# Query projection of the attention split by token half: the second half moved behind the first attention steps

## The chip, the cores and the metric

One core of a Trainium2 chip runs one launch of the kernel. The metric is the device time of that launch in microseconds (us), as the median of several runs. All tensors are float32 in HBM. The engines are called as the profile calls them: PE (TensorE matmul), PEld (its weight load), DVE (VectorE), ACT (ScalarE), POOL (GpSimd) and SP (SyncE, here only an issuer of DMAs). Each engine works through its own queue, and semaphores order the engines against each other.

## What is computed

One encoder block over 1024 tokens of width 1024. A normalised input goes through one projection whose columns feed two mixers: windowed attention (8 query heads, 2 key/value heads, head width 64) and a bidirectional gated DeltaNet (4 heads, width 128, chunks of 64). Both go through one output projection, then a squared-ReLU feed-forward layer follows. Cut to what matters here:

```python
xn = _rmsnorm(h, norm_mix_w)                       # 1024 x 1024
q_a, k_a, v_a, qkv_g, z_g, a_g, b_g = split(xn @ w_in)
attn = _windowed_gqa(q_a, k_a, v_a, bias, in_window, sink)    # each block of 128 queries sees 3 blocks of keys
gdn  = _gdn_mixer(qkv_g, z_g, a_g, b_g, ...)       # inverts 64x64 triangles, then a scan over chunks, both directions
h = h + concat([attn, gdn]) @ w_out
h = h + square(relu(_rmsnorm(h) @ w_ffn_in)) @ w_ffn_out
out = _rmsnorm(h, norm_final_w)
```

The change concerns only when `q_a` (8 heads x 64 = 512 columns, so four column blocks of 128) is computed.

## The kernel before

Float32 precision is had from three matmuls. Each operand is split into a high part that TensorE's float32r type holds exactly and a low remainder; `mm3` (L136 to L138) issues high x high, high x low and low x high into one PSUM bank. A *gemm* below is one column block of 128 by one half of 512 tokens: 8 steps of K by 3 matmuls of 128x512, so 24 matmuls, all into one bank of `psA`. `split` makes the two parts of a weight: ACT casts the high part (L123), POOL subtracts it (L124). `load_w` brings the raw float32 weights as two tiles of `wr`.

SBUF is cut into pools of equal pages: `pg` (24 pages of 4 KB a partition), `dbl` (2 of 8 KB), `sc` and `wr` (4 of 4 KB each), `wh` and `wl` (3 of 4 KB each) and `pt` (12 of 2 KB). PSUM has four banks `psA` and four `psB`. A page is given again to a later tile when its last reader is done, so a tile waits for the page as well as for its data. In the names that the order prints, the last number is the tile's own, the one before it that of the page request (`psA_380_2803`).

The work is written as Python generators, each yielding a rough cost; `weave` takes the next piece from the stream that has used the smallest share of its weight. A scheduler then sets the final order of each engine's queue with a model of its own. On the chip each engine keeps to that order.

Around the change stand these pieces:

- `proj_conv`, `proj_z`, `proj_attn` (first stream of the first weave): the projections. The last eight gemms of `proj_attn` are the queries. For each key/value head `kv`, `pair` gives column block `i` and token `half` in the order (0,0), (1,0), (0,1), (1,1). After each gemm DVE scales the bank into `q` (L509), ACT casts the high part (L510), POOL makes the low part (L511), and SP writes both to a DRAM array `qad` (L513, two writes of 256 KB).
- `query(n, kv)` (L609): SP reads the queries of one block of 128 tokens back from `qad` in the layout that the scores need, two reads of 128 KB.
- `invert` in steps 0 to 3 (the inversion of the triangles): for each step SP loads a `dbl` page from the array `atd` (L721); PE makes products of 32x32 blocks (L738), ACT moves them (L741), PE makes the next ones (L749, L753), DVE and ACT put together `t64` (L758, L763, L765), PE makes 64x64 products from it and the `dbl` page (L774), ACT moves them (L776), PE makes the last products (L782), DVE places them (L785). Copies of the diagonal (L731) go beside it. Steps 0 and 1 stand in the first weave, steps 2 and 3 at the head of the second.
- `bias_table` (L541): 16 DMAs issued from ACT's queue, into `pg` pages that the normalised input held before.
- `attention`: for each block `n` of queries and each `kv`, scores (L556, L557) into four banks of `psA`, DVE adds the bias and takes the maximum (L558), ACT the exponentials (L570), DVE the normalisation (L575); two steps later the transposes (L585), ACT's copies of them (L587) and the products with the values (L597, DVE's copy L600).
- `scan`: the DeltaNet's chunks. Its first products are L820, followed by DVE's L838 and L839. It is woven with the attention.

In `phases` the first weave runs at 145 to 100, and the second, attention and output against inversion and scan, at 100 to 95.

## Time and profile before

| | |
|---|---|
| median of 3 runs | 1226.01 us (1224.49 to 1228.44) |
| the profiled execution: its own time | 1226.09 us |
| its span | 1224.0 us |
| mean granted TensorE clock | 0.989 |
| busy share of the span | PE 96%, DVE 70%, ACT 50%, POOL 46% |
| HBM traffic | 122.39 MB read, 63.49 MB written |

The time is that of the whole launch; the span is from the first to the last event of the profile, 2.1 us less. In rows of the timeline the first number is the start in us from the span's start, the second the duration; `x24` means 24 instructions told in one row, and the bracket says how long the engine had been idle and what released it. The `us` of an issue on a DMA queue (ACTq, SPq) is the queue's time, not that of the transfer. In rows by window, each engine has its busy time and its count of instructions, then follow the granted TensorE clock, the DMA share and GB/s. A PE matmul's busy time is longer than the distance to the next one, as matmuls overlap in the array; distances are told by starts.

### The profile page before, as it was taken

The page shows a single profiled execution, that of the slowest core. Times are in us where ns is not written, and L with a number is a line of the kernel's source. Part 1 is how long each engine was busy: PE and PEld are TensorE (multiplying, and loading weights), DVE is VectorE, ACT ScalarE, POOL GpSimd, SP SyncE. Part 2 cuts the span into 40 slices and gives each one's busy share as a digit, 9 for nine tenths or more (in the row PEclk, how much of TensorE's full clock was granted, in tenths as well). Part 3 has the DMA queues.
Part 4 walks back from the last instruction along what each step waited for, and adds up shares of the span by engine and source line. Part 5 has one row for each costly group of instructions (what it writes and reads, how often), then busy time and mean ns, then how long its engine had stood idle before and what let it go on. Part 6 is the DMA issues. An engine that isn't in the chain of part 4 may idle for free. (4 is left out here: it accounts for less than half of the span.)

```text
span 1224.0 us, 18445 instructions
## 1 busy us (share of the span) xinstructions
PE 1173.7 (96%) x6482; PEld 961.9 (79%) x6482; DVE 855.7 (70%) x1482; ACT 610.4 (50%) x1331; POOL 560.2 (46%) x470
## 2 busy tenths in 40 slices
PE   6999999899889999998999999999999999999997
PEld 5788878687768878887788888888878888888885
DVE  4676667993489996675855454453698796987976
ACT  6455688425376662124755454554555444344443
POOL 5354312224321233232764453635456565565695
PEclk9999999899989999999999999999999999999999
DMA  6134344433645577222144444344789534343323
GB/s 244 52 103 145 92 170 152 162 123 113 207 146 182 157 249 269 76 95 100 56 154 157 146 154 164 130 155 146 240 275 317 200 103 163 131 159 116 103 86 138
DMA packets 121629, 187.62 MB, mean 153 GB/s; under 512 B 11043, under 2 KB 64416, under 8 KB 121537
## 3 DMA queue, kind: packets, MB, share of 16 engines
q1 hardware_dynamic: 103876, 155.20, 38.4%
q10 hardware_dynamic: 17661, 31.24, 6.8%
q8 instruction: 51, 0.84, 0.3%
q14 instruction: 41, 0.34, 0.1%
HBM read 122.39 MB, written 63.49 MB: 152 GB/s over the span
## 5 line engine op out<-in xcount | busy, mean ns | idle before, releaser
L136 PE MATMUL psA<-pg,wh 128*128 128x512 f32 x416 | 165.0, 397 | 2.1 <-ACT pt L473 2.1
L138 PE MATMUL psA<-pg,wl 128*128 128x512 f32 x416 | 164.5, 395 | 0.0
L137 PE MATMUL psA<-pg,wh 128*128 128x512 f32 x416 | 164.2, 395 | 0.0
L124 POOL TENSOR_TENSOR wl<-wr,wh 128x512 fp32r<-128x512 f32 x44 | 66.8, 1540 | 156.5 <-ACT wh L123 128.7
L1194 DVE TENSOR_TENSOR pg<-pg 128x512 fp32r<-128x512 f32 x112 | 124.3, 1145 | 12.9 <-ACT pg L1193 12.9
L124 POOL TENSOR_TENSOR wh<-wr,wh 128x512 fp32r<-128x512 f32 x32 | 47.0, 1487 | 138.2 <-ACT wh L123 138.2
L1111 ACT ACTIVATE pt<-pt 128x512 f32<-128x512 f32 x64 | 40.3, 632 | 122.6 <-DVE pt L1101 122.6
L136 PE MATMUL psA<-pg,pg 128*128 128x512 f32 x256 | 98.7, 391 | 0.9 <-DVE pg L1239 0.9
L137 PE MATMUL psA<-pg,pg 128*128 128x512 f32 x256 | 99.2, 391 | 0.1
L138 PE MATMUL psA<-pg,pg 128*128 128x512 f32 x256 | 99.2, 389 | 0.0
L136 PEld LDWEIGHTS psA<-pg,wh 128*128 128x128 f32 x416 | 78.8, 190 | 19.5 <-ACT pt L473 2.4
L137 PEld LDWEIGHTS psA<-pg,wh 128*128 128x128 f32 x416 | 78.7, 189 | 17.9 <-issue 0.9
L138 PEld LDWEIGHTS psA<-pg,wl 128*128 128x128 f32 x416 | 78.7, 189 | 16.7
L124 POOL TENSOR_TENSOR pg<-wr,pg 128x512 fp32r<-128x512 f32 x48 | 73.2, 1559 | 37.9 <-ACT pg L123 37.9
L1193 ACT CAST pg<-pg 128x512 fp32r<-128x512 f32 x112 | 66.7, 620 | 36.4 <-DMA pg<-sd 31.3
L137 PE MATMUL psB<-pg,pg 128*128 128x512 f32 x192 | 74.9, 390 | 0.8 <-POOL pg L124 0.7
L136 PE MATMUL psB<-pg,pg 128*128 128x512 f32 x192 | 74.7, 389 | 0.0
L138 PE MATMUL psB<-pg,pg 128*128 128x512 f32 x192 | 74.7, 389 | 0.0
L123 ACT CAST wh<-wr 128x512 fp32r<-128x512 f32 x76 | 43.6, 623 | 52.1 <-PE psA L137 31.9
L1101 DVE TENSOR_TENSOR pt<-psB,pt 128x512 f32<-128x512 f32 x39 | 26.9, 690 | 57.6 <-PE psB L138 40.7
L1101 DVE TENSOR_TENSOR pt<-psA,pt 128x512 f32<-128x512 f32 x39 | 26.7, 689 | 51.3 <-PE psA L138 34.1
L136 PEld LDWEIGHTS psA<-pg,pg 128*128 128x128 f32 x256 | 48.0, 188 | 12.1 <-DVE pg L1239 2.1
(395 smaller groups left out, 3234.8 us busy)
## 6 DMA issues: line engine op xcount, KB each, us to landing
sd<-pt ACTq DMA_DIRECT2D x112, 256.0 KB, 2.1
pg<-sd SPq DMA_DIRECT2D x112, 256.0 KB, 2.9
wr<-in_w_ffn_in SPq DMA_DIRECT2D x32, 512.0 KB, 3.6
wr<-in_w_in SPq DMA_DIRECT2D x22, 512.0 KB, 4.2
pg<-in_x SPq DMA_DIRECT2D x16, 512.0 KB, 5.0
wr<-in_w_ffn_out SPq DMA_DIRECT2D x16, 512.0 KB, 4.7
sc<-kvd SPq DMA_DIRECT2D x14, 512.0 KB, 3.7
kvd<-pt SPq DMA_DIRECT2D x16, 256.0 KB, 2.4
```

The lines of the kernel that those rows point to most:

```text
L123: a = nc.scalar.copy(out=h, in_=raw)
L124: b = (eng or nc.gpsimd).tensor_tensor(out=l, in0=raw, in1=h.bitcast(F32), op=ALU.subtract)
L136: nc.tensor.matmul(ps, wh, xh, start=first, stop=False, skip_group_check=onto)
L137: nc.tensor.matmul(ps, wh, xl, start=False, stop=False, skip_group_check=onto)
L138: return nc.tensor.matmul(ps, wl, xh, start=False, stop=last, skip_group_check=onto)
L1101: self.nc.vector.tensor_tensor(out=out, in0=in0, in1=in1, op=ALU.add)
L1111: self.nc.scalar.activation(out=c, in_=c, func=AF.Relu)
L1193: nc.scalar.copy(out=s[:, 0], in_=raw)
L1194: v.tensor_tensor(out=s[:, 1], in0=raw, in1=s[:, 0].bitcast(F32), op=ALU.subtract)
```

## The change

The queries leave `proj_attn` and become `proj_query(half)`. Half 0 (tokens 0 to 511, the four column blocks) stays at the end of the first weave's first stream. Half 1 gets a weave of its own after `bias_table`, at weights 20.8, 14.8 and 18.2, with the inversion steps 2 and 3 and the first 12 pieces of the attention. The inversion steps 2 and 3 leave the head of the scan's stream.

The split weights have to last until half 1 has used them. Block (0,0) is kept in one `dbl` page, high and low part together; block (1,1) has its high part in two `pt` tiles and its low part in `wl`; blocks (0,1) and (1,0) are in `wh` and `wl` as before. Half 1 goes through the blocks in the order (0,0), (1,1), (0,1), (1,0). The number of gemms, casts, subtractions and DMAs of the queries is the same as before. Lines of the kernel before from L541 on stand 23 lines further down in the changed one (L774 is L797, L556 is L579, L820 is L843); the query's own lines L509, L510, L511 and L513 are L532, L533, L534 and L536.

```diff
--- before.py
+++ after.py
@@ -502,18 +502,41 @@
                 pv = self.transposed(t, 0)
                 nc.vector.tensor_copy(out=self.va[:, 4 * half:4 * half + 4, :], in_=pv)
             yield 5.2
-        for kv in range(2):
-            raws = self.load_w(self.w_cols(w, C_AQ + 256 * kv, 256))
-            for i, half, ps in self.pair(raws):
-                q, qh = self.pt(), self.pt(dt=F32R)
-                nc.vector.tensor_scalar(out=q, in0=ps, scalar1=0.125, scalar2=None, op0=ALU.mult)
-                nc.scalar.copy(out=qh, in_=q)
-                nc.gpsimd.tensor_tensor(out=q, in0=q, in1=qh.bitcast(F32), op=ALU.subtract)
-                for part, t in enumerate((qh.bitcast(F32), q)):
-                    nc.sync.dma_start(out=self.qad[kv, part, i, :, half * HALF:(half + 1) * HALF], in_=t)
-                if i == 1 and half == 0:
-                    self.qs.append(self.query(0, kv))
-                yield 5.2
+
+    def proj_query(self, half):
+
+        nc = self.nc
+        if half == 0:
+            self.wq = {}
+        for kv, i in (((0, 0), (0, 1), (1, 0), (1, 1)), ((0, 0), (1, 1), (0, 1), (1, 0)))[half]:
+            if half == 0:
+                if i == 0:
+                    raws = self.load_w(self.w_cols(self.io["w_in"][0], C_AQ + 256 * kv, 256))
+                if (kv, i) == (0, 0):
+                    both = self.dbl((P, 2, NK, P), F32R)
+                    high, low = [both[:, 0, a:a + 4, :] for a in (0, 4)], both[:, 1]
+                elif (kv, i) == (1, 1):
+                    high, low = [self.pt((P, 4, P), F32R) for _ in range(2)], self.wl((P, NK, P))
+                else:
+                    h, low = self.wh((P, NK, P)), self.wl((P, NK, P))
+                    high = [h[:, a:a + 4, :] for a in (0, 4)]
+                for kh in range(2):
+                    self.split(raws[kh][:, :, i * P:(i + 1) * P], high[kh], low[:, 4 * kh:4 * kh + 4, :])
+                self.wq[kv, i] = high, low
+            high, low = self.wq[kv, i]
+            ps = self.ps("psA")
+            for k in range(NK):
+                x = self.xt[half][k]
+                self.mm3(ps, high[k // 4][:, k % 4, :], low[:, k, :], x[:, 0], x[:, 1], k == 0, k == NK - 1)
+            q, qh = self.pt(), self.pt(dt=F32R)
+            nc.vector.tensor_scalar(out=q, in0=ps, scalar1=0.125, scalar2=None, op0=ALU.mult)
+            nc.scalar.copy(out=qh, in_=q)
+            nc.gpsimd.tensor_tensor(out=q, in0=q, in1=qh.bitcast(F32), op=ALU.subtract)
+            for part, t in enumerate((qh.bitcast(F32), q)):
+                nc.sync.dma_start(out=self.qad[kv, part, i, :, half * HALF:(half + 1) * HALF], in_=t)
+            if i == 1 and half == 0:
+                self.qs.append(self.query(0, kv))
+            yield 5.2
 
 
     def bias_rows(self):
@@ -1327,7 +1350,7 @@
         self.kc, self.qc = [None] * 4, [None] * 4
         self.qs = []
         self.wo, self.hnt, self.scanned, self.summed, self.rows = [{}, {}], [None, None], set(), [], {}
-        run(weave((chain(self.proj_conv(C_GV, "v"), self.proj_z(), self.proj_attn()), 145.0),
+        run(weave((chain(self.proj_conv(C_GV, "v"), self.proj_z(), self.proj_attn(), self.proj_query(0)), 145.0),
                   (chain(self.prep(), self.eliminate(), self.diag_blocks(), self.invert(tt, (0, 1))), 100.0)))
         self.bias_table()
 
@@ -1345,9 +1368,10 @@
 
         w_attn = {3: self.load_wout(0, (0,)), 5: self.load_wout(0, (1,)), 7: self.load_wout(0, (3,))}
         w_gdn = {1: self.load_wout(1, (0,)), 2: self.load_wout(1, (1, 2)), 4: self.load_wout(1, (3,))}
-        run(weave((output(), 100.0),
-                  (chain(self.invert(tt, (2, 3)), self.scan(0, tt[0], w_attn), self.load_wout(0, (2,)),
-                         self.scan(1, tt[1], w_gdn)), 95.0)))
+        out = output()
+        run(weave((self.proj_query(1), 20.8), (self.invert(tt, (2, 3)), 14.8), (itertools.islice(out, 12), 18.2)))
+        run(weave((out, 100.0),
+                  (chain(self.scan(0, tt[0], w_attn), self.load_wout(0, (2,)), self.scan(1, tt[1], w_gdn)), 95.0)))
         ng = DFF // 256
         self.norm_half(0)
         cols[1], rest[1] = self.columns(self.load_w1(1), 2)
```

What the scheduler makes of it can be seen in the queues. First PE's queue at inversion step 0. Before:

```order
L753 MATMUL psB_337_2377<-pt_335_2370,sc_327_2298 32x32
L136 MATMUL psA_380_2803<-pg_34_224,wh_378_2797 128x512
...
L138 MATMUL psA_380_2803<-pg_41_245,wl_379_2798 128x512
L774 MATMUL psB_351_2496<-pt_338_2426,dbl_331_2330 64x64 x16
L782 MATMUL psB_353_2515<-pg_332_2332,pt_352_2513 64x64
...
L424 MATMUL psB_358_2567<-ident_84,pt_357_2565 128x128 x4
L738 MATMUL psB_362_2580<-sc_323_2266,dbl_359_2573 32x32
...
L136 MATMUL psA_385_2841<-pg_34_224,wh_383_2835 128x512
```

Now:

```order
L776 MATMUL psB_337_2377<-pt_335_2370,sc_327_2298 32x32
L797 MATMUL psB_351_2496<-pt_338_2426,dbl_331_2330 64x64 x16
L805 MATMUL psB_353_2515<-pg_332_2332,pt_352_2513 64x64
...
L424 MATMUL psB_358_2567<-ident_84,pt_357_2565 128x128 x4
L761 MATMUL psB_362_2580<-sc_323_2266,dbl_359_2573 32x32
...
L136 MATMUL psA_379_2802<-pg_34_224,dbl_378_2797 128x512
```

All 24 matmuls of the first query gemm (`psA_380`) stood between the 32x32 products and the 64x64 products of step 0; now no gemm stands between them, and the first query gemm (`psA_379`, reading its weights from the page `dbl_378`) comes behind the first products of step 1's inversion. The page `dbl_378` is the one that `dbl_331`, step 0's own input, held: its last reader is L797.

Second, SP's queue where the attention's first queries are written and read back; `pt_407` and `pt_401` are the queries of (n 0, kv 1), `pt_428` and `pt_424` those of (n 1, kv 0). Before, the end of the gemms:

```order
L513 DMA qad_78<-pt_406_3014 128x512
L513 DMA qad_78<-pt_405_3013 128x512
L609 DMA pt_407_3020<-qad_78 64x4x128 x2
L513 DMA qad_78<-pt_410_3049 128x512
L513 DMA qad_78<-pt_409_3048 128x512
L609 DMA pt_428_3142<-qad_78 64x4x128 x2
```

Now:

```order
L632 DMA pt_387_2872<-qad_78 64x4x128 x2
L536 DMA qad_78<-pt_394_2911 128x512
L536 DMA qad_78<-pt_393_2910 128x512
L744 DMA dbl_477_3382<-atd_83 128x2x512 x2
L536 DMA qad_78<-pt_400_2950 128x512
L536 DMA qad_78<-pt_399_2949 128x512
L632 DMA pt_401_2956<-qad_78 64x4x128
L632 DMA pt_424_3088<-qad_78 64x4x128
L632 DMA pt_401_2956<-qad_78 64x4x128
```

The writes of the last gemm of half 0 (`pt_400`, `pt_399`) now stand behind the load of `dbl_477`, the input of inversion step 3. Its page is the one that holds the weights of block (0,0), whose last reader is that block's gemm of half 1, the last gemm ahead of the attention. The reads of the queries (0,1) and (1,0) stand behind those writes. Before, two further gemms followed on PE after the writes that the read of (0,1) needs.

Third, PE's queue from the scores of (1,0), `pt_428` before and `pt_424` now, to those of (1,1). Before:

```order
L556 MATMUL psA_440_3202<-pg_342_2444,pt_407_3020 128x256
L557 MATMUL psA_440_3202<-pg_344_2446,pt_407_3020 128x256
...
L556 MATMUL psA_450_3294<-pg_341_2443,pt_428_3142 128x384
...
L557 MATMUL psA_454_3307<-pg_343_2445,pt_428_3142 128x384
L774 MATMUL psB_463_3348<-pt_447_3279,dbl_429_3145 64x64 x16
L585 MATMUL psA_459_3330<-ident_84,wr_419_3108 128x128
L585 MATMUL psA_461_3337<-ident_84,wr_419_3108 128x128
L556 MATMUL psA_467_3369<-pg_342_2444,pt_444_3222 128x384
```

Now:

```order
L579 MATMUL psA_441_3198<-pg_341_2443,pt_424_3088 128x384
...
L580 MATMUL psA_445_3211<-pg_343_2445,pt_424_3088 128x384
L797 MATMUL psB_457_3284<-pt_438_3183,dbl_409_3011 64x64 x10
L608 MATMUL psA_450_3234<-ident_84,wr_415_3054 128x128 x2
...
L608 MATMUL psA_452_3241<-ident_84,wr_415_3054 128x128 x2
...
L797 MATMUL psB_457_3284<-pt_438_3183,dbl_409_3011 64x64
L136 MATMUL psA_454_3248<-pg_63_342,pt_395_2917 128x512
...
L138 MATMUL psA_454_3248<-pg_81_433,wl_397_2919 128x512
L797 MATMUL psB_457_3284<-pt_438_3183,dbl_409_3011 64x64 x5
L579 MATMUL psA_461_3305<-pg_342_2444,pt_435_3126 128x384
```

The gemm of block (1,1), half 1 (`psA_454`, weights in `pt_395` and `wl_397`), stands behind the scores of (1,0) and the first transposes, and its bank is the one of the third of those four scores.

The two gemms left stand further on in the same way: that of block (0,1), 24 matmuls, between the first value product (L620, tiles of n 0) and the scores of (2,0); that of block (1,0) between the scores of (2,1) and the transposes of (1,1), ahead of the last products of inversion step 3 and of the scan's first products (L843).

## The prediction

> **What bounds the kernel now.** I read the page's busy shares first, then windows of the stretch that the change touches, then the engines' timelines there.
>
> ```profile
> span 1224.0 us, 18445 instructions
> PE 1173.7 (96%) x6482; PEld 961.9 (79%) x6482; DVE 855.7 (70%) x1482; ACT 610.4 (50%) x1331; POOL 560.2 (46%) x470
> ```
>
> PE is the bound of the whole, so I ask where PE loses time around the queries, and whether the moved gemms could stand in those holes. Rows by window (length, PE, PEld, DVE, ACT, POOL busy, granted clock, DMA share, GB/s):
>
> ```profile
> 271.60:325.24 53.64, 52.69 (x491) 42.97 (x489) 18.84 (x36) 21.78 (x36) 23.39 (x23) 1.00 0.50 159
> 325.24:361.10 35.86, 28.50 (x545) 23.37 (x543) 29.69 (x105) 30.57 (x77) 9.88 (x12) 0.86 0.39 118
> 330.00:340.00 10.00, 4.58 (x49) 3.91 (x44) 7.47 (x31) 9.90 (x29) 1.70 (x2) 0.68 0.28 75
> 340.00:350.00 10.00, 10.00 (x133) 7.81 (x132) 7.45 (x26) 7.69 (x24) 2.58 (x3) 0.81 0.11 29
> 350.00:360.00 10.00, 8.09 (x164) 6.48 (x162) 9.44 (x32) 9.15 (x21) 1.71 (x3) 1.00 0.59 174
> 370.00:400.00 30.00, 29.44 (x217) 24.99 (x216) 27.96 (x103) 19.97 (x59) 5.62 (x4) 1.00 0.61 192
> ```
>
> The first row runs from the first query gemm to the first scores: PE is idle for 0.95 us of 53.64. The second runs from the first scores to the scan's first product: PE is idle for 35.86 - 28.50 = 7.4 us, and at a mean clock of 0.86 it loses another 0.14 x 35.86 = 5.0 us of array time, 12.4 in all at most, some of it counted in both. So there are holes for about two gemms. But they have an owner: in 350 to 360 DVE is busy 9.44 of 10 and ACT 9.15, and to 400 DVE 27.96 of 30. Behind the first scores it is the softmax's engines that set the pace.
>
> **Prices of the moved work.** The release of the last gemms shows the period and the steps that follow each gemm:
>
> ```profile
> 315.57 0.62 ACT L510 CAST pt<-pt 128x512 fp32r<-128x512 f32 x1 [5.04 <-DMA pg<-biasd]
> 320.91 0.62 ACT L510 CAST pt<-pt 128x512 fp32r<-128x512 f32 x1 [4.72 <-DMA pg<-biasd]
> 325.24 0.28 PE L556 MATMUL psA<-pg,pt 128*128 128x256 f32 x1
> 325.50 0.69 DVE L509 TENSOR_SCALAR pt<-psA 128x512 f32<-128x512 f32 x1 [4.67 <-issue]
> 326.98 1.28 POOL L511 TENSOR_TENSOR pt<-pt,pt 128x512 f32<-128x512 f32 x1 [4.07 <-ACT pt L510]
> 319.55 3.60 SPq L609 DMA_DIRECT2D pt<-qad  x2
> qad<-pt SPq DMA_DIRECT2D x13, 256.0 KB, 2.9
> pt<-qad SPq DMA_DIRECT2D x14, 128.0 KB, 4.5
> DMA to landing us min/median/max: 2.4/4.1/7.6
> ```
>
> One gemm is 320.91 - 315.57 = 5.34, say 5.4 us of PE. It drags DVE 0.69, ACT 0.62, POOL 1.28 and two SP writes along; a write lands after 2.9 us and a read back after 4.5 (medians of 300 to 340 us, by the two rows of issues); the last row is for all transfers of `qad`, writes and reads together. The change keeps the count of all of these. The weights' casts and subtractions are as many as before and go beside gemms, on ACT and POOL that are busy 21.78 and 23.39 of 53.64 us: nothing, as long as gemms cover them.
>
> **First term: inversion step 0 loses its cover.** PE, then ACT, then DVE:
>
> ```profile
> 270.36 0.24 PE L749 MATMUL psB<-sc,pt 32*32 32x32 f32 x4 [0.49 <-ACT pt L741]
> 271.60 0.50 PE L136 MATMUL psA<-pg,wh 128*128 128x512 f32 x1
> 277.27 1.15 PE L774 MATMUL psB<-pt,dbl 64*64 64x64 f32 x32
> 279.11 1.15 PE L782 MATMUL psB<-pg,pt 64*64 64x64 f32 x32 [0.69 <-ACT pt L776]
> 280.77 1.09 PE L738 MATMUL psB<-sc,dbl 32*32 32x32 f32 x64
> 281.79 0.50 PE L136 MATMUL psA<-pg,wh 128*128 128x512 f32 x1
> ...
> 270.20 2.68 ACT L763 COPY pt<-sc 32x256 f32<-32x256 f32 x4
> 272.90 2.69 ACT L731 COPY pg<-sc 32x256 f32<-32x256 f32 x4
> 275.62 1.27 ACT L497 CAST pg<-pt 64x512 fp32r<-64x512 f32 x2
> 276.79 1.25 ACT L498 CAST pg<-pt 64x512 fp32r<-64x512 f32 x2
> 278.47 0.59 ACT L776 COPY pt<-psB 128x512 f32<-128x512 f32 x1 [0.43 <-PE psB L774]
> ...
> 273.73 0.42 DVE L765 TENSOR_SCALAR pt<-psB 32x256 f32<-32x256 f32 x1
> ```
>
> From 271.60 to 277.27 PE now does the first query gemm, and under it ACT and DVE make the operand of L774. The changed order has no gemm there: the first one must wait for its weights' page, which L774's successor (L797) frees. So L797 starts at about 273 and can't end before DVE's last part at 274.15, some 275.3; ACT's copy behind it still stands behind the four casts, which end at 278.04, so the products behind it start at about 278.7. That is 1.4 + 3.4 us of idle PE, and the clock falls after that. The clock's price is seen elsewhere in this trace:
>
> ```profile
> 906.50 0.50 PE L136 MATMUL psB<-dbl,sc 128*128 128x512 f32 x1 [2.08 <-ACT pt L1106]
> 907.10:910.40 3.30, 3.30 (x9) 2.62 (x8) 2.57 (x5) 2.85 (x6) 1.28 (x1) 0.50 1.04 389
> ```
>
> An idle of 2.08 us was followed by a stretch of some 3.3 us at a granted clock of 0.50. I take 1.4 us for it here. Then L805, the transposes and L761 take from 278.7 to 281.6, with the clock to 283.0, where the first gemm starts. Before, the second began at 281.79. The deficit is 5.4 + 1.2 = 6.6 us. [...]
>
> Three gemms later PE meets a second new wait: the weights of block (1,1) are cast only behind the third gemm's own cast in ACT's queue. Gemm end, 0.69 + 0.62 + one cast of 0.62 make about 1.9 us. So five gemms end, and the first scores start, at 283.0 + 5 x 5.4 + 1.1 (inversion step 2's first products, done early) + 0.6 (a small rest of step 1) + 1.9 + small losses, which I put at 317.6: 7.6 us before the old 325.24, with three gemms, 16.2 us, still owed. If nothing of these were hidden, the kernel would be 16.2 - 7.6 - 1.1 = 7.5 us slower; if the whole 12.4 of the holes took them, 4.9 faster.
>
> **Second term: the attention's start.** The rows that set it before:
>
> ```profile
> 335.62 0.45 PE L774 MATMUL psB<-pt,dbl 64*64 64x64 f32 x2 [3.93 <-ACT pt L763]
> 339.84 0.67 PE L556 MATMUL psA<-pg,pt 128*128 128x384 f32 x1
> 348.88 0.44 PE L556 MATMUL psA<-pg,pt 128*128 128x384 f32 x1
> 349.52 2.00 DVE L575 TENSOR_SCALAR wr<-wr,nm 128x384 f32<-128x384 f32 x3
> 359.96 1.75 DVE L575 TENSOR_SCALAR wr<-wr,nm 128x384 f32<-128x384 f32 x3
> 361.11 1.16 PE L820 MATMUL psB<-sc,pg 128*128 128x128 f32 x8
> ```
>
> The hole that a gemm could fill is the 3.93 us ahead of L774. In the new order it opens sooner and a gemm doesn't fill it. The reads of query (0,1) were issued at 319.55, under two further gemms that covered write, landing, read and landing. Now the last gemm of half 0 ends just ahead of the first scores; from 317 on DVE 0.69, ACT 0.62 and POOL 1.28 make its parts, the write lands 2.9 later, the read 4.5 after that: 317 + 0.7 + 0.6 + 1.3 + 2.9 + 4.5 = 327.0, and SP has the load for step 3 ahead of them. The scores of (0,1) then start at 327.4, those of (1,0) at about 330.5 and the gemm behind them at 334, since its bank is freed by DVE's pass over the third of those scores. So PE stands nearly idle from about 319 to 327, more than in the hole it had. That gemm ends at 334 + 5.4 = 339.5, and the scores of (1,1) follow, which stood at 339.84 before. Everything gained by starting 7.6 us early is used up: -0.3 us, with one gemm done and two owed. From both sides: with landings between the shortest, 2.4 us, and the medians that I used, and some delay of DVE, the gemm starts between 331.5 and 335, so -2.8 to +0.7.
>
> **Third term: the two gemms left, 10.8 us.** One stands ahead of the scores (2,0), which began at 348.88, the other ahead of the transposes before the scan. DVE is the engine to be fed there, at 9.44 of 10. While PE does a gemm, DVE can only live on what it already has. At 348.88 that was about L575's 2.00 and the 0.69 of a value copy; of 5.4 + 0.7 us until the new scores DVE then starves some 3.4. At the second it has more, an L575 of 1.75 and the bias pass of the last scores, and starves some 2. The three gemms' own evictions add 3 x 0.69 = 2.1 to DVE. Sum +7.5; ends +2.1 (no starving) and +10.8 (no cover). I take 7.5 since DVE had at most 0.6 us of slack per 10 there.
>
> **Fourth term: the clock behind the hole.** The 330 to 350 rows with 0.68 and 0.81 say that about 3.2 + 1.9 = 5.1 us of array time went at half rate. Of it some 2 us fell behind 339.84. The new hole comes earlier; the clock is back for the scores (1,1), but the gemm at 334 may run part of its time at half rate. I take -2.0 + 1.3 = -0.7, with -2 and +0.7 as ends.
>
> **The sum.** -0.3 + 7.5 - 0.7 = +6.5 us at the scan's start, which is 6.5 against the 7.5 of nothing hidden. From there to 400 DVE has 2 us of slack in 30, so little is won back, and the queues behind are those of before. On the profiled execution's own 1226.09 us that is 1232.6; the median of the runs, 1226.01, is 0.08 away, so no correction: 1232.5.
>
> **Rivals.**
>
> *Holes filled (faster).* The mechanism is the gemms taking the place of waiting in the attention's first steps. It decides at the third term: if DVE's backlog covers both gemms (third term +2.1), the gemm of (1,1) starts at 331.5 (-2.8) and the half clock goes (-2.0), the sum is -2.7; and if PE's 12.4 us can all be taken, -4.9: about 1222. For it speaks the 7.4 us of idle PE. Against it: PE's order is fixed, and each gemm stands ahead of scores that DVE waits for, not beside them. The point is 7.5 us hidden of the 16.2.
>
> *Little difference.* The third term at about half, +4, with -2.8 from quick landings: +1 us or so, 1227. For it speaks that DVE's queue holds work of three attention steps at once; against it the 0.69 us evictions, which are sure.
>
> *Wait for the queries worse than priced (slower still).* SP's step 3 load, ACT's bias DMAs and the writes share the queues' order. If the reads land at 7.6 us, the longest of this trace, 3 us more are lost ahead of the gemm: 1235.5, and up to 1239 with both gemms bare.
>
> *The change doesn't move anything* is excluded: the queues show the moved gemms.
>
> **How the numbers follow.** A median of three runs that spread over 1224.49 to 1228.44 can't tell less than about 0.3%, 3.7 us, from no change. My forecast with its sizes, and the worse wait, are slower by more than that: 0.44 and 0.12. The cases between -3.7 and +3.7 get 0.25, the filled holes 0.19. So faster 0.19, same 0.25, slower 0.56. The range reaches down to 1219, below the filled holes' 1222 by the size of one landing, and up to 1239; the likeliest case alone would be 1229 to 1237.
>
> **What would show it.** First: no gemm at 271.6, two idles and a granted clock of 0.50 near 276 to 283, the first gemm at about 283. Second: first scores at 316 to 319, then idle PE until the scores of (0,1) at 326 to 328, released by the read from `qad`; the gemm of (1,1) at 332 to 335. Third: DVE idle ahead of the bias passes of (2,0), and the scan's first product at 366 to 371 in place of 361.11. I am wrong if that product comes before 363, if the DVE doesn't starve beside the two late gemms, or if the time is lost or won behind 400.

## Result, and the profile after

| kernel | median us | runs | ratio to before, 95% interval |
|---|---|---|---|
| before | 1227.22 | 4 | |
| changed | 1248.12 (1247.09 to 1251.05) | 4 | 1.0172 (1.0156 to 1.0188) |

The change costs about 21 us. The forecast was 1232.5 us with a range to 1239: the direction was right, the size a third. The profiled execution of the changed kernel took 1251.05 us, 3 us above the median; its trace is 25 us longer than that of before, and that is the difference accounted for below. So some 4 us of it belong to that execution rather than to the change.

The page's busy shares of the changed kernel, same columns as before:

```profile
span 1249.0 us, 18445 instructions
PE 1185.5 (95%) x6482; PEld 967.6 (77%) x6482; DVE 858.9 (69%) x1482; ACT 610.0 (49%) x1331; POOL 559.1 (45%) x470
```

As many instructions as before on every engine, and DVE, ACT and POOL are within 3.2 us of their old busy times. PE alone is busy 11.8 us longer with the same 6482 matmuls. Now both traces cut at the same events: inversion step 0, the first scores, the scores of (1,1), the scan's first product, a cut in the feed-forward part, and the end. Rows by window (length, PE, PEld, DVE, ACT, POOL busy, granted clock, DMA share, GB/s), before:

```profile
268.80:325.24 56.44, 55.00 (x649) 45.07 (x649) 20.39 (x40) 24.46 (x41) 25.58 (x24) 1.00 0.51 165
325.24:339.84 14.60, 9.18 (x220) 7.91 (x218) 11.54 (x46) 12.46 (x32) 4.61 (x6) 0.79 0.41 125
339.84:361.11 21.27, 19.33 (x328) 15.46 (x326) 18.16 (x60) 18.11 (x46) 5.28 (x6) 0.91 0.38 113
361.11:640.00 278.89, 265.50 (x1572) 221.76 (x1569) 212.22 (x547) 132.88 (x341) 108.25 (x95) 0.99 0.46 152
640.00:1215.90 575.90, 571.82 (x2490) 466.49 (x2488) 394.77 (x471) 268.91 (x476) 321.48 (x228) 1.00 0.48 162
```

And changed:

```profile
268.50:318.92 50.42, 43.89 (x641) 35.73 (x641) 16.39 (x33) 21.66 (x37) 18.64 (x18) 0.86 0.35 107
318.92:345.29 26.37, 15.82 (x186) 13.06 (x184) 15.17 (x54) 13.00 (x37) 8.69 (x10) 0.74 0.50 152
345.29:379.80 34.51, 30.92 (x370) 23.12 (x368) 22.81 (x65) 21.89 (x53) 10.37 (x10) 0.90 0.34 112
379.80:664.90 285.10, 270.77 (x1570) 225.00 (x1567) 211.37 (x542) 130.50 (x332) 105.80 (x93) 0.98 0.46 150
664.90:1240.80 575.90, 571.14 (x2491) 465.38 (x2489) 394.60 (x471) 269.62 (x476) 320.73 (x228) 1.00 0.48 162
```

The last row is the same in both, 575.90 us. In the four rows ahead of it the length grows from 371.2 to 396.4, by 25.2 us. PE's idle time (length less busy) grows from 22.2 to 35.0, by 12.8; PE's busy time grows from 349.0 to 361.4, by 12.4, for the same work. By this account the loss is half waiting, half the same matmuls at a lower granted clock, and it lies in all four stretches. The account says where PE's time went; it doesn't say what the time would be at full clock, since a PE that does its matmuls faster may only wait longer.

The hole behind the first scores, on PE, ACT and SP of the changed kernel:

```profile
329.19 0.28 PE L772 MATMUL psB<-sc,pt 32*32 32x32 f32 x4 [8.84 <-ACT pt L764]
331.96 0.55 PE L579 MATMUL psA<-pg,pt 128*128 128x256 f32 x1 [1.71 <-DMA pt<-qad]
...
319.42 5.45 ACTq L564 DMA_DIRECT2D pg<-biasd  x5
324.90 1.28 ACT L590 ACT_TABLE_LOAD   x1 [4.89 <-DMA dbl<-atd]
328.77 0.36 ACT L764 COPY pt<-psB 128x256 f32<-128x256 f32 x1
...
320.09 1.62 SPq L536 DMA_DIRECT2D qad<-pt  x2
327.69 1.91 SPq L632 DMA_DIRECT2D pt<-qad  x3
```

Two waits end within 3 us of each other. ACT's five bias issues take 5.45 us, and the last of them goes out at 324.6, right behind the landing of step 3's input. That load was issued at 319.12, behind the last reader of the page with block (0,0)'s weights. The exponentials and the copy for step 2 stand behind ACT's issues. And the queries (0,1) are written at 320 to 321.7, read from 327.7 and landed at 331.9.

In the changed kernel's trace the granted clock stood at 0.50 for 10.24 us from 272.03, 3.41 from 306.16, 13.65 from 323.23 and 6.83 from 350.53. Rows of three pairs of neighbouring stretches of that trace:

```profile
347.12:350.53 3.41, 1.49 (x31) 1.21 (x30) 2.85 (x11) 3.17 (x6) 0.55 (x1) 1.00 0.58 192
350.53:353.95 3.42, 3.09 (x76) 1.99 (x76) 2.02 (x5) 3.41 (x13) 0.17 (x1) 0.50 0.02 5
...
538.27:541.68 3.41, 1.49 (x8) 1.11 (x8) 3.41 (x8) 1.24 (x2) 1.85 (x2) 1.00 0.40 131
541.68:545.09 3.41, 3.14 (x10) 2.66 (x11) 2.92 (x7) 0.62 (x1) 1.80 (x2) 0.50 0.27 104
...
272.03:275.45 3.42, 1.84 (x28) 1.71 (x30) 2.51 (x6) 3.34 (x6) 0.31 (x1) 0.50 0.29 80
275.45:278.86 3.41, 1.30 (x24) 1.12 (x22) 0.00 (x0) 3.36 (x7) 2.68 (x3) 0.50 0.00 0
```

Each of the two stretches in which PE was busy 1.49 us of 3.41 is followed by one at 0.50, and the one at 0.50 with 1.84 us busy by another at 0.50. No single idle in these stretches was longer than 2.10 us.

### The profile page after: what moved, and what is told of

The parts are those of the page before. It is cut to its first block, busy times and chain, and to the rows that moved or that the text cites. A ratio compares the mean times of both kernels' runs of the same rounds, so it can differ in the third digit from the quotient of the medians.

```text
span 1249.0 us, 18445 instructions
## 1 busy us (share of the span) xinstructions
PE 1185.5 (95%) x6482; PEld 967.6 (77%) x6482; DVE 858.9 (69%) x1482; ACT 610.0 (49%) x1331; POOL 559.1 (45%) x470
## 5 line engine op out<-in xcount | busy, mean ns | idle before, releaser
L138 PE MATMUL psA<-pg,wl 128*128 128x512 f32 x400 | 158.3, 396 | 0.0
L136 PE MATMUL psA<-pg,wh 128*128 128x512 f32 x384 | 152.8, 399 | 2.1 <-ACT pt L473 2.1
L137 PE MATMUL psA<-pg,wh 128*128 128x512 f32 x384 | 151.6, 395 | 0.0
L124 POOL TENSOR_TENSOR wl<-wr,wh 128x512 fp32r<-128x512 f32 x40 | 61.5, 1559 | 150.5 <-ACT wh L123 127.1
L138 PEld LDWEIGHTS psA<-pg,wl 128*128 128x128 f32 x400 | 75.7, 189 | 16.2
L136 PEld LDWEIGHTS psA<-pg,wh 128*128 128x128 f32 x384 | 72.9, 190 | 19.8 <-ACT pt L473 2.4
L137 PEld LDWEIGHTS psA<-pg,wh 128*128 128x128 f32 x384 | 72.9, 190 | 16.7 <-issue 0.9
```

The costliest lines, as they stand in the source:

```text
L124: b = (eng or nc.gpsimd).tensor_tensor(out=l, in0=raw, in1=h.bitcast(F32), op=ALU.subtract)
L136: nc.tensor.matmul(ps, wh, xh, start=first, stop=False, skip_group_check=onto)
L137: nc.tensor.matmul(ps, wh, xl, start=False, stop=False, skip_group_check=onto)
L138: return nc.tensor.matmul(ps, wl, xh, start=False, stop=last, skip_group_check=onto)
```

## Experiments

All ratios are to the kernel before on the same chip. The median beside each is that of its own runs.

**Order by halves alone, nothing late.**

```diff
- chain(..., self.proj_attn(), self.proj_query(0))          # first weave
+ chain(..., self.proj_attn(), self.proj_query(0), self.proj_query(1))
- run(weave((self.proj_query(1), 20.8), (self.invert(tt, (2, 3)), 14.8), (islice(out, 12), 18.2)))
- run(weave((out, 100.0), (chain(self.scan(...)...
+ run(weave((out, 100.0), (chain(self.invert(tt, (2, 3)), self.scan(...)...
```

> Only the order by halves and the new places of the weights are kept: all eight gemms stand ahead of the attention again, the inversion steps 2 and 3 at the head of the scan's stream. Theory A (three separate losses: about 8.6 us of PE until the first scores, of which 6.6 at inversion step 0; about 7.6 us in the hole behind the first scores; the rest behind it): only the first is left, 1233 us, with no gemm at step 0 and no wait above 5 us behind the first scores. Theory B (nearly all comes from the attention's start, the hole at step 0 is made up later): 1227 to 1229 us.

1235.84 us, ratio 1.0078 (1.0050 to 1.0106). The first scores start at 337.7 in place of 325.2; behind them the distance to the scan's first product is 35.0 us against 35.9. So the order by halves and the new places of the weights cost 9.5 us before a single gemm is late. That is theory A's side, with a first loss larger than its 6.6 and a time 3 us above its 1233.

**Step 0 covered again.** The double page goes to block (0,1); block (0,0) is in `wh` and `wl`.

```diff
- if (kv, i) == (0, 0):                      # takes the double page
+ if (kv, i) == (0, 1):
- ((0, 0), (1, 1), (0, 1), (1, 0)))[half]
+ ((0, 1), (1, 1), (0, 0), (1, 0)))[half]
```

> The changed kernel, but block (0,1) is kept in the double page and block (0,0) in wh and wl, so that the first query gemm has its weights without waiting for step 0's page. The queue of PE behind it is nearly that of the changed kernel. Theory A: the 24 matmuls stand at step 0 again, the idle and the half clock there go, 6 us less than the changed kernel, 1241 to 1242 us. Theory B: the first scores start 6 us sooner but the hole behind them grows by as much, 1247 us. A third way, that the page rather than the place matters: less than 3 us.

1246.71 us, ratio 1.0176 (1.0134 to 1.0217): no gain that could be told. The gemm is back at step 0, but the first scores start only 3.3 us earlier (315.6), and the hole behind them stands as it was (7.9 + 2.3 us). The time is that of the third way of its expectation, and of theory B too; the trace speaks for the third, since the hole didn't grow and PE waits 3.8 us for step 2's input ahead of the first scores.

**The same cover, with all gemms ahead**, tells what took its place.

> The order by halves with all eight gemms ahead of the attention, as in the first run, but block (0,1) in the double page and block (0,0) in wh and wl, so that the first gemm is at inversion step 0 again. If the 9.5 us of the first run are the bare step 0 with its idle and half clock, they go but for about 1.5 us of the new wait for the casts of block (1,1): 1226 to 1229 us. If they come from the places of the weights or from the queries' order otherwise: 1232 us or more.

1232.45 us, ratio 1.0036 (1.0017 to 1.0055): by the ratios 5 of the 9.5 us come back, 4.4 don't. The time is at the edge of the expectation's second case (1232 or more, by the places of the weights), though about half came back as the first case had it. PE's waits in this kernel between step 0 and the first scores (us in all, times, longest):

```profile
PE psB L761 <- DMA dbl<-atd: 4.8, 2, 2.8
PE psB L805 <- ACT pt L799: 1.0, 2, 0.7
```

PE waits 4.8 us for step 2's input from DRAM, a wait that the kernel before doesn't have. With one of the two `dbl` pages holding weights from step 0 until the first gemm of half 1, the inversion has one page left, and its next load starts only when the step before has read its own. So the double page costs the inversion its second buffer. In the changed kernel itself PE has no such wait ahead of the first scores (step 2's input is issued at 296.14 and first used at 303.66); there the page shows as step 0's lost cover and as the late load of step 3.

**One and two gemms late instead of three.** `late` is the generator of half 1, of which one or two pieces more are run ahead of the weave.

```diff
+ late = self.proj_query(1)
+ run(itertools.islice(late, 1))              # 2 in the second run
- run(weave((self.proj_query(1), 20.8), ...
+ run(weave((late, 20.8), ...
```

> The changed kernel, but the second gemm of half 1, block (0,0) being the first, is put ahead of the attention: its generator is run one piece ahead of the weave, which puts two of the four gemms of half 1 (blocks (0,0) and (1,1)) ahead of the first scores. Two gemms stay behind. Theory A (the hole behind the first scores is a wait for queries written, read back and for ACT, which a gemm in that place covers): 5 us less than the changed kernel, 1243 us. Theory C (what costs is each gemm that stands ahead of scores that DVE waits for, some 5 us for each): 1243 us too, but the hole stays and the late gemms get cheaper. The trace tells: the wait ahead of the scores of (0,1), 11.9 us in the changed kernel, is below 7 by A and above 10 by C.

> As the run with one piece ahead, with two pieces: three gemms of half 1 stand ahead of the first scores, only block (1,0) stays behind. Theory A: the hole behind the first scores falls to the old one, about 3.9 us, and what is left is step 0 and one late gemm: 1234 to 1236 us. Theory C: 1237 to 1239 us, about 5 us below the run with one piece ahead.

With two late gemms 1242.22 us (1.0127; 1.0098 to 1.0156), with one 1236.31 (1.0078; 1.0050 to 1.0105). In a row: none late 1235.8, one 1236.3, two 1242.2, three 1248.1. With two late the time fits theory A and theory C alike (1243); its trace fits A, since PE waits 4.0 us ahead of the scores of (0,1), not above 10. With one late it is between the two. The first scores start at 327.8, 324.3 and 318.9 with one, two and three late, but the scores of (1,0) at 334.7, 334.2 and 334.4: they are pinned. In all three PE waits there for queries from `qad`: 2.2 us ahead of (1,0) with one late, 4.0 and 1.7 us ahead of (0,1) with two and three. A gemm taken from ahead of the first scores makes those start earlier, not the next ones; so the first is free, and each further one costs 5.9 us, its own 5.4 and a little.

And one gemm late with step 0 covered:

> As the run before this one, but with the last gemm of half 1 left behind the first scores and the inversion steps 2 and 3 in the weave of the changed kernel. One gemm behind the scores was worth +0.5 us with the bare step 0, so 1227 to 1230 us; below 1224 only if a single late gemm fills the old hole of 3.9 us.

1233.82 us, ratio 1.0054 (1.0032 to 1.0077), no better than with none late and the same cover (1232.45), and above its expectation for the same reason, the wait for step 2's input (1.6 + 3.2 us in its trace).

**The late gemms cut to one step of K.**

```diff
+ nk = 1 if half == 1 and (kv, i) != (0, 0) else NK
- for k in range(NK):
+ for k in range(nk):
```

> The changed kernel, but the three gemms of half 1 that stand behind the first scores do one step of K only, 3 matmuls in place of 24, some 4.7 us of PE less each (part of the queries is left out); what follows each gemm is kept. If these gemms are bare where they now stand (theory C), 14 us less, 1234 us. If half of them is hidden in PE's holes, 7 us less, 1241 us. If the holes take them whole, 1246 to 1248 us. Theory A, by which the early start gains nothing, needs the first of these.

1235.74 us, ratio 1.0067 (1.0043 to 1.0091): 12.4 us less than the changed kernel for some 14 us of PE taken away. That is the first case of its expectation: the late gemms were nearly bare where they stood.

**The two waits of the hole.** Bias tables in 4 DMAs from an array of 128 stored rows a head:

```diff
- self.biasd = d("biasd", (8, 32, 512))
+ self.biasd = d("biasd", (8, P, 512))
- for m in range(4): ...  ap=[[511, 32], [32 * 512, 2], [1, 3 * P]]
+ ap=[[511, P], [P * 512, 2], [1, 3 * P]]
```

> The changed kernel, but the attention's bias tables come in 4 DMAs of ACT's queue rather than 16, from an array of bias rows that is stored four times as often; the result is the same. In the changed kernel the last of the 16 was issued only when the load of step 3's input had landed, at 324.9 us, and ACT's exponentials and the copy that step 2's products wait for stood behind it. Theory A1 (ACT held by these issues is the floor behind the first scores): step 2's products start at 323 to 325 us rather than 329.2 and the time falls by 4 to 5 us to 1243 to 1244. Theory A2 (the floor is the queries' way through DRAM): the products start sooner too, but the scores of (0,1) stay at 331 to 332 us and the time falls by less than 1.5 us.

1257.34 us, ratio 1.0250, slower. The larger array spoiled the test: PE lost 9.9 us in one wait that ended at 183.4 us. From PE's waits of that run (us in all, times, longest) and DVE's timeline:

```profile
PE psB L674 <- DVE pt L683: 9.9, 1, 9.9
...
182.26 1.12 DVE L683 SCALAR_TENSOR_TENSOR pt<-pt,cc,psB 128x128 f32<-128x128 f32 x4 [12.09 <-DMA biasd<-pt]
```

DVE's L683, for which PE waits, was itself released by the landing of that write, issued at 139.3. The write's source is a tile of `pt`, and L683 writes a tile of `pt`: so it most likely waited for the source's page. SP's other issues were slow in that stretch too (two loads of weights took 19.95 us of its queue, 5.56 in the changed kernel). The next run's expectation put the loss down to SP's queue, so there the write goes out from POOL's:

> The changed kernel with 4 bias DMAs of ACT's queue, as before, but the larger array of bias rows is written from POOL's queue: written from SP's it held SP's other transfers for some 10 us at 144 to 190, which hid what was asked. Theory A1 (ACT held by the issues): counted from the first scores to the end, 4 us less than the changed kernel, 1243 to 1245 us. Theory A2: less than 1.5 us. If the write still holds other transfers, the time is above 1250 us and only the stretch behind the first scores can be compared.

1258.64 us, ratio 1.0255, against 1257.34 and 1.0250 with the write on SP's queue: another queue didn't help. In both only the stretch behind can be compared: from the first scores to the scan's first product it is 58.5 us, against 60.9 in the changed kernel. By that ACT's hold is worth 2.5 us, which two spoiled runs suggest but don't show.

The queries of three steps from an array written long before (other values, same work):

```diff
+ arr = self.ktd[2 * kv:2 * kv + 2] if 0 < 2 * n + kv < 4 else self.qad[kv, part]
- src = self.qad[kv, part, :, :, n * P:(n + 1) * P]...
+ src = arr[:, :, n * P:(n + 1) * P]...
```

> The changed kernel, but the queries of (0,1), (1,0) and (1,1) are read from an array of equal shape that was written long before (the keys of the other mixer), so that these reads wait for no write; the values are others, the work is the same. Theory A1: the scores of (0,1) start right behind those of (0,0), but the exponentials and step 2's products stay at about 329 us, less than 2 us gained. Theory A2: 4 to 5 us gained, 1243 to 1244 us. If neither wait alone is the floor, both this run and the one with 4 bias DMAs gain little, and both together gain 6 us or more.

1239.95 us, ratio 1.0097 (1.0065 to 1.0129): 8.2 us less than the changed kernel, more than any theory gave. The scores of (0,1) start at 325.9 rather than 332.0. The stretch from the first scores to the scan is 55.4 us, 5.5 shorter. The clock goes with it: PE's rows are 14.40 busy of 24.10 us at 0.86 from the first scores to (1,1), and the next stretch to the scan runs wholly at 1.00. The first scores start 1.8 us earlier, which the edit doesn't touch; so the 8.2 is not all its own.

```profile
317.10:341.20 24.10, 14.40 (x185) 11.85 (x183) 14.82 (x54) 13.19 (x37) 8.73 (x10) 0.86 0.55 167
341.20:372.50 31.30, 28.55 (x373) 22.32 (x369) 22.65 (x65) 22.32 (x53) 10.40 (x10) 1.00 0.37 123
```

Both edits together:

> The changed kernel with both: 4 bias DMAs and the three early queries read from the array written long before. Theory A (the hole behind the first scores is made of these two waits, each hiding the other): the hole of 8.8 us goes to below 4, the gemm of block (1,1) starts at 330 to 333 us rather than 339.1, and the time is 1240 to 1242 us. Theory C (the hole only moves, since DVE and ACT need the time and each late gemm costs its 5 us wherever it stands): 1245 us or more.

1252.56 us, ratio 1.0204, with the same spoiled start; from the first scores to the scan 56.7 us, against 55.4 with the early queries alone. So the queries' way through DRAM was the main floor (A2).

**The clock alone.** 30 matmuls that no result uses, behind the bias passes of the first scores:

```diff
+ idle = self.ps("psB")
+ nc.tensor.matmul(idle[:, 0:4], self.ident, mx, start=True, stop=True)
+ for _ in range(30):
+     nc.tensor.matmul(idle, self.kh[0][:, 0:P], self.kh[0][:, 0:HALF], start=True, stop=True)
```

> The changed kernel with 30 matmuls of 128x512 added that no result uses, ordered behind the bias passes of the first scores, where PE is idle for 8.8 us. Theory D (half of the loss is the clock: between 268.5 and 664 us the changed kernel has 11.0 + 6.4 us of PE time lost at half rate against 3.3 + 1.5 before): the stretch at half rate from 323.2 to 336.9 goes, 3 us less, 1244 to 1246 us, though PE does 6.8 us more. Theory E (the clock costs nothing of its own, ACT and DVE pace these stretches): no less than 1247.5 us, and more if the added work delays the next products.

1245.00 us, ratio 1.0147 (1.0125 to 1.0169), 3.1 us less than the changed kernel though PE does 6.8 us more. The three stretches to the scan:

```profile
268.50:316.60 48.10, 40.88 (x593) 33.11 (x583) 16.93 (x32) 20.80 (x36) 18.73 (x18) 0.93 0.36 112
316.60:343.00 26.40, 23.05 (x218) 19.01 (x217) 15.17 (x53) 12.98 (x37) 8.35 (x9) 0.87 0.49 153
343.00:376.80 33.80, 30.13 (x370) 22.63 (x368) 22.85 (x65) 22.27 (x53) 10.63 (x10) 0.95 0.35 114
```

The clock there is 0.87 and 0.95 where it was 0.74 and 0.90, and the time is the one that theory D named. But the two rows that the added work touches are together only 0.7 us shorter than in the changed kernel (26.40 and 33.80 against 26.37 and 34.51), and the first row, which it doesn't touch, is 2.3 us shorter at a clock of 0.93 against 0.86. The intervals of the two ratios overlap as well. So it isn't shown that the half rate behind the first scores costs time of its own: the row in which the clock rose most, from 0.74 to 0.87, kept its length.

**Late gemms that take no page.** The kernel before, by columns, with its last gemms left out of the first weave; `wh` and `wl` hold their weights anyway.

```diff
+ attn = self.proj_attn()
- chain(..., self.proj_z(), self.proj_attn())
+ chain(..., self.proj_z(), itertools.islice(attn, 12 - late))         # late = 0, 1 or 2
- run(weave((output(), 100.0), (chain(self.invert(tt, (2, 3)), self.scan(...)...
+ out = output()
+ run(weave((islice(out, 3), 3.9), (self.invert(tt, (2,)), 7.4), (attn, 5.2)))  # 5, 6.5 and 10.4 with two
+ run(weave((out, 100.0), (chain(self.invert(tt, (3,)), self.scan(...)...
```

> The control for the two runs with late gemms: the same weave, the first three pieces of the attention with inversion step 2, then the rest, with no gemm moved. If the weave alone does nothing, 1226 to 1228 us; what the runs with one and two gemms give is to be read against this one.

> The kernel before, order by columns, weights in wh and wl as before; only the last query gemm is left out of the first weave and woven with the first three pieces of the attention and inversion step 2. It comes behind the scores of (0,0) and ahead of those of (0,1). No page is taken from the inversion. Theory F (the double page, not the moving, is what costs at the inversion; the hole behind the first scores is 3.9 us idle and about 3.4 us of half rate, and one gemm fills part of it): 1222 to 1226 us, no wait for the inversion's input from DRAM. Theory C (each gemm put behind the scores costs its 5 us): 1231 us.

> The same with the last two gemms, over five pieces of the attention; one comes behind the scores of (0,0), one behind step 2's 64x64 products, ahead of the first transposes. Theory F: within 3 us of the run with one gemm; theory C: 5 us above it, 1236 us. The first scores start 10.8 us earlier than in the kernel before where nothing else changes.

The weave alone: 1239.41 us (1.0089; 1.0064 to 1.0114), 11 us slower than before, a control that was not neutral (its PE waits 5.5 us ahead of step 2's last products). One gemm late: 1236.02 (1.0074; 1.0049 to 1.0098). Two: 1224.06 (0.9968; 0.9952 to 0.9984). Neither theory had that: F put two within 3 us of one, C 5 us above. The control differs from the run with two in its weave as well (three pieces of the attention against five), so the 15 us between them can't be put down to the gemms. Against the kernel before, two late gemms in this order cost nothing. Its rows to the scan:

```profile
268.50:311.60 43.10, 39.72 (x514) 32.14 (x515) 18.97 (x34) 21.40 (x36) 20.36 (x20) 0.96 0.41 134
311.60:340.10 28.50, 25.87 (x296) 21.52 (x294) 18.32 (x62) 15.39 (x40) 10.39 (x11) 0.94 0.54 164
340.10:359.60 19.50, 16.93 (x311) 13.06 (x309) 15.27 (x46) 15.80 (x37) 4.65 (x6) 0.91 0.46 149
```

The first scores start at 311.6, 13.6 us earlier than before, but the scores of (1,1) at 340.1 (339.8 before) and the scan at 359.6 (361.1): the gemms moved into idle time that the earlier start opened, and nothing behind came sooner. To see whether the small gain is real, and whether the place counts (the second run below is the same kernel with `(attn, 5.2)` in place of 10.4):

> The same kernel as the run with two late gemms, to narrow its interval. If the gain is real, the ratio to the kernel before stays at 0.995 to 0.999; if it was the draw of the runs, 0.999 to 1.002.

> Two late gemms as before, but the second one further back: behind the scores of (2,0) rather than ahead of the first transposes. Theory C (a gemm ahead of scores and transposes that wait costs its time): 2 to 5 us slower than the other place, 1226 to 1229 us. If DVE's backlog covers it there, the same time.

Again 1225.36 us, ratio 0.9988 (0.9976 to 1.0001); further back 1227.24, 0.9996 (0.9981 to 1.0012). Two gemms late are free there. The two runs of the one kernel, 22 executions, both lie below 1, by 0.3% and 0.1%, and the second is in the band that its expectation gave to a real gain; one of the two intervals reaches 1, so a gain of some 2 us is likely, not shown. The place of the second gemm makes 1.9 us between the medians and 0.0008 between the ratios, whose intervals overlap: theory C's 2 to 5 us and no difference can't be told apart.

## Why the prediction was right and wrong

The sign and the route of the first three terms held; the sum was a third of the loss. What failed is the size of the second and third terms, the clock term, and the nothing that was set behind the scan's start.

*First term, inversion step 0.* Its times were right: the first gemm was forecast at 283.0 and starts at 282.09, the first scores at 317.6 and start at 318.92; the wait for block (1,1)'s cast, 1.9, is 1.73. PE's timeline of the changed kernel there:

```profile
272.84 0.44 PE L797 MATMUL psB<-pt,dbl 64*64 64x64 f32 x2 [1.43 <-DVE pt L788]
274.06 1.94 PE L797 MATMUL psB<-pt,dbl 64*64 64x64 f32 x30 [0.77 <-DVE pt L788]
278.10 1.98 PE L805 MATMUL psB<-pg,pt 64*64 64x64 f32 x32 [2.10 <-ACT pt L799]
282.09 0.57 PE L136 MATMUL psA<-pg,dbl 128*128 128x512 f32 x1
...
306.48 0.79 PE L136 MATMUL psA<-pg,pt 128*128 128x512 f32 x1 [1.73 <-ACT pt L123]
307.50 0.63 PE L136 MATMUL psA<-pg,dbl 128*128 128x512 f32 x1
313.26 0.39 PE L138 MATMUL psA<-pg,wl 128*128 128x512 f32 x1
```

The parts that the term names add up to 313.6, and 4.0 us to 317.6 are called small losses without a row. Before, the stretch from 281.79 to 325.24 took 5.7 us beyond its seven gemms of 5.4, which is what the 1.1, the 0.6 and the 4.0 make together; so the size was right, but it wasn't shown. A price that the term didn't have is the page: with the cover restored the inversion's next load waits for it, 4.8 us.

*Second term, the attention's start: -0.3 forecast, +5.5 measured* (scores of (1,1) at 345.29, before 339.84). The route was right, write and read through DRAM, and the sizes were medians of a quiet stretch: 2.9 for the writes, where the read could only be issued 6.0 us after the last write's issue, with the bias and step 3 transfers under way at the same time; then 4.3 for the read. The term reached 327.4, the trace 331.96. Its bounds went down to the shortest landing and hardly up, though the same row gave 7.6 as the longest; that case was told as a rival with 0.12 and priced at 3 us. It was the nearest of the rivals: with both gemms bare it reached 1239. One more thing lies ahead of it, in the rows above: PE began the last gemm of half 0 at 306.48, turned after two matmuls to the gemm of block (0,0), half 1, and took the first one up again at 313.26. Its low weights come from a subtraction of POOL's that ended at 309.7. So its result, for which the queries (0,1) wait, came only at 318. No run here tries it the other way round.

*Third term, the two late gemms: +7.5, measured 13.2* (34.51 against 21.27 us from the scores of (1,1) to the scan). DVE starves ahead of (2,0) for 5.26 us, where 3.4 was forecast, and behind the second gemm's start for 2.48, where 2 was; from DVE's timeline of the changed kernel:

```profile
362.83 0.69 DVE L532 TENSOR_SCALAR pt<-psA 128x512 f32<-128x512 f32 x1 [5.26 <-PE psA L138]
376.60 0.16 DVE L594 TENSOR_TENSOR nm<-nm,nm 128x4 f32<-128x4 f32 x1 [2.48 <-ACT pg L593]
```

My own upper end, 10.8 for two bare gemms, was the right value; the 5.9 us for each further gemm in the series says so too. The rest of the 13.2 is PE's idle, 3.6 against 1.9, and 0.8 us more of busy time, with 6.8 us at half rate against 4.0. So DVE's backlog, which was to cover 3.3 of the 10.8, covered nothing: the scan's first product came at 379.8, not at 366 to 371.

*Fourth term, the clock: -0.7 and the 1.4 of the first term, measured +7.1 us of PE's busy time up to the scan's start, and +5.3 behind it.* This measure lies inside the lengths given for the other terms and doesn't come on top of them. I took one idle of 2.08 us and one stretch of 3.3 us behind it as the price of a hole. In the trace the clock fell at 272.0, before any idle of that size: PE had been idle for 0.49 us and for the first 0.6 of the 1.43. It stayed at 0.50 for 10.2 us, over idles of 1.43, 0.77 and 2.10 us; it was down for 3.4 more at 306.2, for 13.7 behind the first scores and for 6.8 at 350.5. How much of the loss would go at full clock stays open: the run with added matmuls didn't show it. No idle at 272 to 282 or at 347 was longer than 2.10 us, and the clock fell at both.

*Behind the scan's start: 0, measured +6.2* (the row that ends at 664.90 is 285.10 us long against 278.89), some of it behind 400, which the prediction named as a sign of being wrong. PE is busy 5.3 us longer in it and idle 0.9 longer; the clock is at half for 13.7 us there (from 541.7, 582.6 and 627.0), before for 3.4. Why PE's short idles there met more slow stretches is open. Part of it is the draw of that execution, whose time lies 3 us above the median.

*The rival of filled holes* was wrong for this kernel, but not because gemms can't fill holes, as I argued: by columns, with no page taken, two did. It was the hole itself that grew at its front, as the series with the pinned scores of (1,0) shows.

## What to carry to other kernels

Deferring work helps only where what it delayed is not pinned by something else: here the next scores hung on the last query's write and read back, so the early start only opened a longer hole. Count a page that has to live longer against the buffer it is taken from, also where nobody waits for it yet. And where PE is the bound, compare its busy time for the same instructions, not only its idle time: here the one grew by 12.4 us and the other by 12.8, at a granted clock of 0.86 against 1.00 in the first row. That names a suspect; what it costs needs a run of its own.

## What the runs showed of the hardware

In the changed kernel's trace the granted clock fell from 1.00 to 0.50 at 272.03, 306.16, 350.53 and 541.68 us, among other places; in the 3.41 us ahead of these four PE had been busy for 2.30, 2.00, 1.49 and 1.49 us. In the trace of before, 1.50 us of 3.41 stood ahead of the fall at 333.60, while 1.87 of 3.40 from 434.60 was followed by a stretch at 1.00. At 0.50, a stretch with 3.09 us busy from 306.16 was followed by one at 1.00, and one with 3.09 from 350.53 by another at 0.50. These are single cases of two traces; they don't give one busy time at which the clock falls or comes back.

In the run with 4 bias DMAs (1257.34 us) a write of 2 MB that repeats 8 rows 128 times each was issued from SP's queue at 139.31 us. The DVE instruction that its landing released, behind 12.09 us of idle, started at 182.26, 42.95 us after the issue. That the write held its source's page until then is inferred from that release. With the write on POOL's queue the kernel took 1258.64 us.
